# Six added split places at stage ends, no GpSimd split at mix2's entries, and a reordered first expert round

## The chip, the cores and the metric

The kernel runs on one core of a Trainium2 chip. The metric is the device time of one execution in microseconds. The kernel before takes 2223.85 us (median of 3 runs, 2223.41 to 2227.16).

## What is computed

Two blocks, one after the other, on 256 tokens of 1024 features in float32, each of depth 2.

```python
def first_block(x, mem, ...):
    for l in range(DEPTH):
        h = rms_norm(x, ffn1_norms[l, 0])
        x = x + 0.5 * rms_norm(swiglu(h, ffn1_w13[l], ffn1_w2[l]), ffn1_norms[l, 1])
        h = rms_norm(x, mix_norms[l, 0])
        y = token_mixing(h, w_in[l], ...)
        x = x + rms_norm(y, mix_norms[l, 1])
        h = rms_norm(x, cross_norms[l, 0])
        x = x + rms_norm(cross_attention(h, m, ...), cross_norms[l, 1])
        h = rms_norm(x, ffn2_norms[l, 0])
        x = x + 0.5 * rms_norm(swiglu(h, ffn2_w13[l], ffn2_w2[l]), ffn2_norms[l, 1])
def second_block(x, c, ...):
    for l in range(DEPTH):
        mod = (c_act @ w_ada[l] + b_ada[l])[:, None, :]
        shift_m, scale_m, gate_m, shift_f, scale_f, gate_f = jnp.split(mod, N_MOD, axis=-1)
        h = rms_norm_2(x, norm_mix[l]) * (1.0 + scale_m) + shift_m
        x = x + gate_m * hybrid_mixer(h, w_in[l], ...)
        h = rms_norm_2(x, norm_ffn[l]) * (1.0 + scale_f) + shift_f
        x = x + gate_f * hierarchical_moe(h, ...)   # 4 groups x 8 experts, top 2 of one group
```

## The kernel before

The tokens are two tiles of 128, t=0 and t=1. The stages follow one another: ffn1, mix, cross and ffn2 for each layer, then mix2 and the experts for each layer. A float32 product is three matmuls (`mm3`, L303 to L305): each operand is split into a high and a low half, and high x high, high x low and low x high are added up.

**Weights.** `Stream` holds a stage sequence's weights in the order of their use. `load` sends them over SP's queue, 1 MB each, into four buffers raw0 to raw3. `pump` splits them in pieces of 128x512 into places: ACT writes the high half (L288 with the norm's gain folded in, L291 without), DVE the low half (L289, L293), or GpSimd, at L293 too, where a key's third field is true and the piece's number is odd. There are eight places (SPLITS): four tiles "hl" and two tiles "pair" that hold two each. `take` hands out the next split piece after pumping as many as there are places; `release` gives a place back, and `taken` gives a raw buffer back, upon which `load` sends the next transfer. A new split needs a free place, so what may be split ahead is limited by the eight.

**The end of a stage.** `finish` calls `dense_out`, the stage's last product, and `boundary`. `dense_out` works through items of one weight piece each (six matmuls, three per tile): first the head, all but the last eight, for both tiles; then the eight tail pieces for t=0, and, handed out by `rest(n, pump)`, for t=1. In `boundary` tile 0's residual add and norm (`add_post`: L506, L508, L511) stand beside those matmuls of tile 1. Then comes `staggered`: the next stage's first product, one pass of 24 matmuls for t=0 (`run(0)`, L373 and L375), tile 1's transposes (`out_of(1)`, L446), and the same for t=1 (`run(1)`). The eight pieces for it are taken in `run(0)`; their places are released in `run(1)`. Where a gain can be folded into the weights (five ends: ffn1 to mix and cross to ffn2 in both layers, and ffn2 to ffn1 between them) x itself is transposed; else `pre_norm` makes h first (L521, L524, L529).

**mix2's entries.** `mix2_keys` marks the first two keys with True, so half of their eight low halves are written by GpSimd (eight instructions in the kernel).

**Adaptation rows.** `ada_step` sums a row of 1024 on DVE, and `close` reduces it over the partitions with two matmuls of 512 columns and adds the bias on DVE (L1342).

**Experts.** `moe` works in eight rounds q of four experts. A round gathers the tokens (L1951, evicted by ACT at L1956 and DVE at L1958), multiplies with gate and up weights (`gate_up`, L1964), weighs the result, transposes it (L2007, L2009) and multiplies with the down weights (L2021); `ymoe` (L2026) puts the rows back. Its weights come unsplit through SP's queue; transfers wait for the buffers that the gate/up and down matmuls give back (issued at L1726). The routing weights per slot come from `comb`: 16 matmuls of four columns, for all rounds, after the first round's gate/up (L1987). A float32 matmul of the expert stages leaves two records in the trace.

Of the kernel before, what the change touches and what calls it, by code (L numbers as in the profile page):

```python
# [35 lines left out]
SPLITS = 8  # L36
# [131 lines left out]
class Stream:  # L168
# [3 lines left out]
    def __init__(self, kern, keys, limit=None):  # L172
        self.kern, self.keys = kern, list(keys)
        self.raws, self.ready = [], deque()
# [4 lines left out]
        self.emitted = 0  # L179
        self.load(limit)  # L180
# [73 lines left out]
class Kernel:  # L254
# [106 lines left out]
    def staggered(self, keys, lhs):  # L361

        outs = self.mm("first")
        parts = []
        te = self.nc.tensor

        def run(t):
            for k0 in (0, 4):
                if t == 0:
                    parts.extend(self.st.take(*keys[k0 // 4]) for _ in range(4))  # L370
                for k in range(k0, k0 + 4):
                    for i in range(2):
                        te.matmul(outs[t], lhs(k, t)[0], parts[k][i], start=(k == 0 and i == 0), stop=False)  # L373
                for k in range(k0, k0 + 4):
                    te.matmul(outs[t], lhs(k, t)[1], parts[k][0], start=False, stop=(k == 7))  # L375
                    if t == 1:
                        self.st.release()
                        self.st.pump(1)

        return outs, run  # L380

    def dense_out(self, keys, lhs, tail, closing=None, mid=(), ada=None, halves=False):
# [131 lines left out]
    def pre_norm(self, x, g, sh, junk, h):  # L514
# [16 lines left out]
    def boundary(self, ys, rest, post, gp, gn, first=None, filler=None):  # L531
# [13 lines left out]
        def pre_of(t):  # L545
# [5 lines left out]
            elif gn is not None:  # L551
                self.pre_norm(self.x[t], gn[0], gn[1], *tiles[t])
# [15 lines left out]
        rest(1, 1)  # L568
        post_of(0)
        rest(1, 1)  # L570
# [6 lines left out]
        else:  # L577
            pre_of(0)
            rest(2, 2)
# [3 lines left out]
        self.st.pump(2)  # L583
# [736 lines left out]
    def ada_step(self, l, i, k, fp):  # L1320
# [4 lines left out]
        def rows():  # L1325
            bn = self.A("bn")
            for g in range(2):
                p, c0 = slice(32 * g, 32 * g + 32), g * 512
                nc.sync.dma_start(bn[p, 0, :], self.a["b_ada"][l, i * D + c0:i * D + c0 + 512].unsqueeze(0)
                                  .to_broadcast([32, 512]))  # L1330
                if gain:
                    nc.sync.dma_start(bn[p, 1, :], self.a[gain][l, c0:c0 + 512].unsqueeze(0).to_broadcast([32, 512]))
            return bn

        def close(acc, bn):

            tp = self.tp("adap")
            for g in range(2):
                nc.tensor.matmul(tp[32 * g:32 * g + 32, :], self.ones[:, 0:32], acc[:, g * 512:(g + 1) * 512],
                                 start=True, stop=True)  # L1340
            row = fp.tile([64, 512], F32, tag="row", name="row")
            nc.vector.tensor_add(row, tp[0:64, :], bn[0:64, 0, :])  # L1342
            if gain:
                nc.vector.scalar_tensor_tensor(row, row, 1.0, bn[0:64, 1, :], op0=ALU.add, op1=ALU.mult)
            for g in range(2):
                c0 = i * D + g * 512
                nc.sync.dma_start(self.mod_dram[l:l + 1, c0:c0 + 512], row[32 * g:32 * g + 1, :])
# [64 lines left out]
    def mix2_keys(self, l):  # L1412
        keys = [("win2", (l, i), True) for i in range(2)] + [("wlr", (l,), False)]
# [419 lines left out]
    def moe(self, l, hm, L, pre):  # L1833
        nc, a, tc = self.nc, self.a, self.tc
        te, ve = nc.tensor, nc.vector
        with self.moe_ctx as es:
# [78 lines left out]
            def one_round(ahead):  # L1915
# [28 lines left out]
                def gather(q, cuts=((0, 4), (4, 8)), xg=None):  # L1944
# [24 lines left out]
                with tc.manual_schedule(engines=ORDERED) if ahead else nullcontext():  # L1969
                    places(0, 4)  # L1970
                    xg = gather(0, {0: ((0, 1), (1, 2)), 1: ((2, 4),), 3: ((4, 8),)}[0])
                    for k in range(8):
# [10 lines left out]
                        if k == 7:  # L1983
                            comb_tp = self.tp("comb")
                            for i in range(8):
                                for t in range(2):
                                    te.matmul(comb_tp[:, i * 4:(i + 1) * 4], P[t][:, i * 128:(i + 1) * 128],  # L1987
                                              comb[:, t, i * 4:(i + 1) * 4], start=(t == 0), stop=(t == 1))
                            cw, cs = r2.tile([128, 8, 4], F32, name="cw"), r2.tile([128, 8], F32, name="cs")
                            ve.tensor_mul(cw, comb_tp[:, 0:32].rearrange("p (q e) -> p q e", q=8),  # L1990
                                          self.misc[:, 34:38].unsqueeze(1).to_broadcast([128, 8, 4]))
                            ve.reduce_sum(cs, cw, AX.X)
                for q in range(8):
# [10 lines left out]
                    ve.scalar_tensor_tensor(sil, sil, cs[:, q:q + 1], gu[:, 256:512], op0=ALU.mult, op1=ALU.mult)  # L2004
# [9 lines left out]
                    nc.scalar.activation(PT, tp[:, 256:512].rearrange("p (f s) -> p f s", f=2), AF.Copy)  # L2014
                    dn = self.mm("dn")
# [102 lines left out]
```

## Time and profile before

| | before |
|---|---|
| median of 3 runs | 2223.85 us |
| the profiled execution | 2221.21 us |
| its span | 2219.2 us |
| PE busy | 2108.2 us (95%) |
| DVE busy | 1350.9 us (61%) |
| ACT busy | 1157.7 us (52%) |
| GpSimd (POOL) busy | 68.4 us (3%) |
| HBM read | 549.85 MB, 248 GB/s over the span |

All durations are those of the profiled execution. Its own time is 2 us more than its span, for what lies around the span, and 2.6 us below the median. An engine's busy time counts its instructions from start to end; idle time in the timeline stands in brackets with what ended it.

### The profile page before, as it was taken

What the parts mean: (1) busy time and instruction counts of PE and PEld (TensorE: products, weight loads), DVE (VectorE), ACT (ScalarE), POOL (GpSimd) and SP (SyncE); (2) the same over time, 40 slices, a digit from 0 to 9 for tenths busy, and PEclk for the clock granted to TensorE, in tenths of its full rate; (3) what the DMA queues carried; (4) which work ended last, traced back from release to release, by engine and by line L of the source; (5) the groups of instructions that cost most, each with busy time, mean ns of one, the idle gap of its engine ahead of it and who ended that gap; (6) DMA issues with size and microseconds to landing.
All of it is one profiled execution on the core that took longest, in us unless ns stands there. A gap on an engine that the chain in (4) does not pass through costs nothing. (4 is left out here: it accounts for less than half of the span.)

```text
span 2219.2 us, 28887 instructions
## 1 busy us (share of the span) xinstructions
PE 2108.2 (95%) x10668; PEld 1561.2 (70%) x10668; DVE 1350.9 (61%) x2472; ACT 1157.7 (52%) x2196; POOL 68.4 (3%) x76
## 2 busy tenths in 40 slices
PE   8999999999999999999999999998999887998895
PEld 7887878888788788777788878876765333775341
DVE  6876767765787687676677558766562114563111
ACT  6555677565655555466766556545842112762110
POOL 0000000000000000000000000002000001100000
PEclk9999999999999999999999999999999898999998
DMA  7875534553687577744356437766489998569998
GB/s 290 315 246 203 191 117 168 192 194 128 218 286 240 201 277 260 261 169 152 133 182 225 152 126 276 261 248 242 152 315 380 418 418 331 220 240 370 418 417 338
DMA packets 94551, 552.96 MB, mean 249 GB/s; under 512 B 11223, under 2 KB 12954, under 8 KB 41398
## 3 DMA queue, kind: packets, MB, share of 16 engines
q1 hardware_dynamic: 94398, 550.99, 67.0%
q8 instruction: 88, 1.44, 0.3%
q14 instruction: 65, 0.53, 0.1%
HBM read 549.85 MB, written 1.10 MB: 248 GB/s over the span
## 5 line engine op out<-in xcount | busy, mean ns | idle before, releaser
L289 DVE SCALAR_TENSOR_TENSOR hl<-raw,g_pre,hl 128x512 fp32r<-128x512 f32 (+1 forms) x296 | 214.2, 744 | 46.1 <-ACT hl L288 45.6
L288 ACT ACTIVATE hl<-raw,g_pre 128x512 fp32r<-128x512 f32 (+1 forms) x296 | 204.5, 719 | 62.4 <-PE gu L305 24.9
L289 DVE SCALAR_TENSOR_TENSOR pair<-raw,g_pre,pair 128x512 fp32r<-128x512 f32 (+1 forms) x296 | 207.6, 744 | 46.1 <-ACT pair L288 43.5
L293 DVE TENSOR_TENSOR hl<-raw,hl 128x512 fp32r<-128x512 f32 (+1 forms) x286 | 192.7, 688 | 68.8 <-ACT hl L291 65.5
L288 ACT ACTIVATE pair<-raw,g_pre 128x512 fp32r<-128x512 f32 (+1 forms) x296 | 196.6, 715 | 71.8 <-PE gu L305 52.0
L291 ACT ACTIVATE hl<-raw 128x512 fp32r<-128x512 f32 (+1 forms) x290 | 176.9, 626 | 94.3 <-PE y L305 41.1
L1964 PE MATMUL gu<-raw,xg 128*32 128x512 f32 x1024 | 144.0, 633 | 25.2 <-DMA raw<-w_gu 23.0
L293 DVE TENSOR_TENSOR pair<-raw,pair 128x512 fp32r<-128x512 f32 (+1 forms) x184 | 119.8, 692 | 69.7 <-ACT pair L291 69.3
L291 ACT ACTIVATE pair<-raw 128x512 fp32r<-128x512 f32 (+1 forms) x188 | 107.4, 621 | 91.6 <-PE y L305 64.3
L303 PE MATMUL gu<-pair,hh 128*128 128x512 f32 x320 | 127.3, 398 | 0.0
L303 PE MATMUL gu<-hl,hh 128*128 128x512 f32 x320 | 126.3, 395 | 0.0
L305 PE MATMUL gu<-pair,hl 128*128 128x512 f32 x320 | 125.1, 391 | 0.0
L305 PE MATMUL gu<-hl 128*128 128x512 f32 x320 | 125.0, 391 | 0.0
L304 PE MATMUL gu<-pair,hh 128*128 128x512 f32 x320 | 124.8, 390 | 0.0
L304 PE MATMUL gu<-hl,hh 128*128 128x512 f32 x320 | 124.8, 390 | 0.0
L1359 DVE SCALAR_TENSOR_TENSOR ada<-raw,cact,ada 128x512 f32<-128x512 f32 x168 | 122.0, 745 | 0.0
L1964 PEld LDWEIGHTS gu<-raw,xg 128*32 128x32 f32 x1024 | 29.8, 112 | 107.2 <-DMA raw<-w_gu 52.9
L1951 PEld LDWEIGHTS gather<-P,u 128*128 128x128 f32 x512 | 69.0, 214 | 30.3 <-issue 21.3
L2021 PE MATMUL dn<-raw,aT 128*32 128x512 f32 x512 | 79.2, 623 | 10.2 <-DMA raw<-w_dn 3.0
L2004 DVE SCALAR_TENSOR_TENSOR sil<-sil,cs,gu 128x256 f32<-128x256 f32 x16 | 7.7, 481 | 124.0 <-ACT sil L2003 123.7
L298 DVE TENSOR_TENSOR y<-dn,y 128x512 fp32r<-128x512 f32 x32 | 22.1, 692 | 98.5 <-ACT y L297 98.4
L1956 ACT ACTIVATE xg<-gather,fm 128x128 f32<-128x128 f32 x64 | 29.2, 457 | 95.4 <-PE gather L1951 80.6
(672 smaller groups left out, 4879.3 us busy)
## 6 DMA issues: line engine op xcount, KB each, us to landing
raw<-w SPq DMA_DIRECT2D x131, 1024.0 KB
raw<-w_gu SPq DMA_DIRECT2D x98, 1024.0 KB
raw<-win SPq DMA_DIRECT2D x71, 1024.0 KB
raw<-w_dn SPq DMA_DIRECT2D x54, 1024.0 KB
raw<-w_ada SPq DMA_DIRECT2D x48, 1024.0 KB
raw<-w_gu SPq DMA_DIRECT2D x60, 512.0 KB
raw<-w_out SPq DMA_DIRECT2D x16, 1024.0 KB
raw<-cross_wkv SPq DMA_DIRECT2D x16, 1024.0 KB
```

Of the source, the lines that this page charges most:

```text
L288: nc.scalar.activation(hi, raw[:, c0:c0 + n], AF.Copy, scale=gain)
L289: nc.vector.scalar_tensor_tensor(lo, raw[:, c0:c0 + n], gain, hi.bitcast(F32), op0=ALU.mult, op1=ALU.subtract)
L291: nc.scalar.activation(hi, raw[:, c0:c0 + n], AF.Copy)
L293: eng.tensor_tensor(out=lo, in0=raw[:, c0:c0 + n], in1=hi.bitcast(F32), op=ALU.subtract)
L303: te.matmul(out, xh, wh, start=start, stop=False)
L304: te.matmul(out, xh, wl, start=False, stop=False)
L305: te.matmul(out, xl, wh, start=False, stop=stop)
L1359: nc.vector.scalar_tensor_tensor(self.ada[:, c], w, act, self.ada[:, c], op0=ALU.mult, op1=ALU.add)
L1951: te.matmul(ps[:, (k - k0) * 128:(k - k0 + 1) * 128], hm[t][:, k * 128:(k + 1) * 128], P[t][:, q * 128:(q + 1) * 128], start=(t == 0), sto ...
L1956: nc.scalar.activation(xg[:, k, :], v, AF.Identity, bias=sh, scale=g)
L1964: te.matmul(gu[32 * e:32 * e + 32, :], xg[:, k, 32 * e:32 * e + 32], w(e), start=(k == 0), stop=(k == 7))
L2021: te.matmul(dn[half][32 * e:32 * e + 32, :], aT[:, f, 32 * e:32 * e + 32], w(e), start=(f == 0), stop=(f == 1))
```

## The change

It consists of five parts.

1. In the last six head items of a stage that has a next stage's first product (`AHEAD`), each item allows one extra split place, a tile "ahead" from the pool "ap". It serves the five folded ends and the entry of mix2 in layer 0. During the pass for t=0 (`held`) `take` pumps no more than it needs.
2. In `boundary` the numbers handed to `pump` move: fewer pieces between the residual instructions, one piece ahead of h's scaling, and all that is missing of eight ahead of x[1]'s last add where nothing is folded.
3. The first two keys of mix2 are no longer marked for GpSimd.
4. `ada_step` closes a row in four groups of 256 columns on 128 partitions instead of two of 512 on 64.
5. In `moe` the comb matmuls are made round by round (two each), the next round's gather is emitted after the transposes are evicted instead of before them, and one eviction of the first gather goes to ACT.

```diff
-SPLITS = 8
+SPLITS, AHEAD = 8, 6
...
     def slot(self, i):
...
+        if self.extra:
+            self.extra -= 1
+            self.used.append(None)
+            return self.kern.ap.tile([128, 2, 512], F32R, tag="A", name="ahead").rearrange("p a b -> p (a b)")
...
     def take(self, name, index):
-        self.pump()
+        self.pump(SPLITS if not self.held else 0 if self.ready else 1)
...
         def run(t):
+            self.st.held = t == 0
...
-        for k, c in items[:head]:
+        for i, (k, c) in enumerate(items[:head]):
+            if i >= head - ahead:
+                self.st.extra += 1
...
     def pre_norm(self, x, g, sh, junk, h, between=None):
...
+        if between:
+            between()
         for c in HALF:
...
         post_of(0)
-        rest(1, 1)
+        rest(1, int(fold))
         post_of(0)
-        rest(1, 1)
+        rest(1, int(fold))
...
         else:
-            pre_of(0)
-            rest(2, 2)
+            pre_of(0, lambda: self.st.pump(1))
+            rest(2)
             rest(4)
             post_of(1)
             out_of(0)
-        self.st.pump(2)
+        if fold or ys is None:
+            self.st.pump(2)
+        else:
+            self.st.pump(8 - len(self.st.ready))
         post_of(1)
...
-        ys, rest = self.dense_out(keys, lhs, tail, closing, mid, ada, experts)
+        ys, rest = self.dense_out(keys, lhs, tail, closing, mid, ada, experts, 0 if kw.get("first") is None else AHEAD)
...
-            for g in range(2):
-                nc.tensor.matmul(tp[32 * g:32 * g + 32, :], self.ones[:, 0:32], acc[:, g * 512:(g + 1) * 512],
+            for g in range(4):
+                nc.tensor.matmul(tp[32 * g:32 * g + 32, 0:256], self.ones[:, 0:32], acc[:, g * 256:(g + 1) * 256],
                                  start=True, stop=True)
-            row = fp.tile([64, 512], F32, tag="row", name="row")
-            nc.vector.tensor_add(row, tp[0:64, :], bn[0:64, 0, :])
+            row = fp.tile([128, 256], F32, tag="row", name="row")
+            nc.vector.tensor_add(row, tp[:, 0:256], bn[:, 0, 0:256])
...
-        keys = [("win2", (l, i), True) for i in range(2)] + [("wlr", (l,), False)]
+        keys = [("win2", (l, i), False) for i in range(2)] + [("wlr", (l,), False)]
...
-                            if k % 2 == 0:
+                            if k % 2 == 0 or (first and k == 1):
...
-                        if k == 7:
-                            comb_tp = self.tp("comb")
-                            for i in range(8):
-                                for t in range(2):
-                                    te.matmul(comb_tp[:, i * 4:(i + 1) * 4], P[t][:, i * 128:(i + 1) * 128],
-                                              comb[:, t, i * 4:(i + 1) * 4], start=(t == 0), stop=(t == 1))
...
-                    if q < 7:
-                        xg = gather(q + 1)
+                    ctp, cw, cs = self.tp("comb"), r2.tile([128, 4], F32, name="cw"), r2.tile([128, 1], F32, name="cs")
+                    for t in range(2):
+                        te.matmul(ctp[:, 0:4], P[t][:, q * 128:(q + 1) * 128], comb[:, t, q * 4:(q + 1) * 4],
+                                  start=(t == 0), stop=(t == 1))
+                    ve.tensor_mul(cw, ctp[:, 0:4], self.misc[:, 34:38])
+                    ve.reduce_sum(cs, cw, AX.X)
...
                     nc.scalar.activation(PT, tp[:, 256:512].rearrange("p (f s) -> p f s", f=2), AF.Copy)
+                    if q < 7:
+                        xg = gather(q + 1)
                     dn = self.mm("dn")
```

**How the rows move.** The first place is DVE at the end of ffn1 in layer 0, before the change (x_85 and x_86 are x for t=0 and t=1; g_pre marks the next stage's weights; y is the last product).

```order
L293 TENSOR_TENSOR hl<-raw,hl 128x512 x3
L506 TENSOR_TENSOR u<-y_1287,gain 128x512
L464 TENSOR_SCALAR rs_tmp<-ms 128x1
L508 TENSOR_TENSOR u<-y_1288,gain 128x512
L511 SCALAR_TENSOR_TENSOR x_85<-u,rs,x_85 128x512 x2
L289 SCALAR_TENSOR_TENSOR pair<-raw,g_pre,pair 128x512 x3
L298 TENSOR_TENSOR hl<-tp,hh 128x512 x2
L506 TENSOR_TENSOR u<-y_1289,gain 128x512
L464 TENSOR_SCALAR rs_tmp<-ms 128x1
L508 TENSOR_TENSOR u<-y_1290,gain 128x512
L289 SCALAR_TENSOR_TENSOR pair<-raw,g_pre,pair 128x512
L289 SCALAR_TENSOR_TENSOR hl<-raw,g_pre,hl 128x512
```

The same place in the changed kernel, from one extra place on to the first pair of x_86:

```order
L298 TENSOR_TENSOR ahead<-raw,ahead 128x512
L294 SCALAR_TENSOR_TENSOR hl<-raw,g_pre,hl 128x512
L1356 TENSOR_TENSOR row<-adap,bn 128x256
L294 SCALAR_TENSOR_TENSOR ahead<-raw,g_pre,ahead 128x512
L294 SCALAR_TENSOR_TENSOR hl<-raw,g_pre,hl 128x512
L294 SCALAR_TENSOR_TENSOR ahead<-raw,g_pre,ahead 128x512
L294 SCALAR_TENSOR_TENSOR hl<-raw,g_pre,hl 128x512 x2
L515 TENSOR_TENSOR u<-y_1301,gain 128x512
L473 TENSOR_SCALAR rs_tmp<-ms 128x1
L517 TENSOR_TENSOR u<-y_1302,gain 128x512
L520 SCALAR_TENSOR_TENSOR x_85<-u,rs,x_85 128x512 x2
L294 SCALAR_TENSOR_TENSOR pair<-raw,g_pre,pair 128x512 x2
```

Before, the eight splits of the next stage (g_pre) all stand behind x_85's add, the last three behind x_86's. Now six of them stand ahead of the first `u`, and two behind x_85's add.

The second place is PE in the first round of the experts. Before, 16 comb rows and 14 gather rows stand ahead of these:

```order
L1951 MATMUL gather<-P_14179,u 128x128
L1951 MATMUL gather<-P_14180,u 128x128
L2007 MATMUL actT<-ident,sil 128x128 x2
L2009 MATMUL actT<-ident,P_14179 128x128
L2009 MATMUL actT<-ident,P_14180 128x128
L1964 MATMUL gu<-raw,xg 32x512 x5
L2021 MATMUL dn_14341<-raw,aT 32x512 x8
L1964 MATMUL gu<-raw,xg 32x512 x4
L2026 MATMUL ymoe_14181<-y,PT 128x512
```

In the changed kernel two comb rows and nine gather rows stand ahead of these:

```order
L1965 MATMUL gather<-P_14268,u 128x128
L1965 MATMUL gather<-P_14267,u 128x128
L2015 MATMUL actT<-ident,sil 128x128 x2
L2017 MATMUL actT<-ident,P_14267 128x128
L2017 MATMUL actT<-ident,P_14268 128x128
L1965 MATMUL gather<-P_14268,u 128x128
L1965 MATMUL gather<-P_14267,u 128x128
L1965 MATMUL gather<-P_14268,u 128x128
L1965 MATMUL gather<-P_14267,u 128x128
L1965 MATMUL gather<-P_14268,u 128x128
L2031 MATMUL dn_14415<-raw,aT 32x512 x8
L1978 MATMUL gu<-raw,xg 32x512
```

The four transposes now come in the middle of the gather, and the first down matmuls (dn) stand directly behind it; the gate/up matmuls that stood around them come later.

The third place is DVE at the entry of mix2 in layer 0, before the change (hl and pair from raw are the splits; h is what PE transposes).

```order
L511 SCALAR_TENSOR_TENSOR x_85<-u,rs,x_85 128x512 x2
L293 TENSOR_TENSOR pair<-raw,pair 128x512
L521 TENSOR_TENSOR h<-x_85,gain 128x512
L464 TENSOR_SCALAR rs_tmp<-ms 128x1
L524 TENSOR_TENSOR h<-x_85,gain 128x512
L529 SCALAR_TENSOR_TENSOR h<-h,rs,gain 128x512 x2
L293 TENSOR_TENSOR pair<-raw,pair 128x512
L506 TENSOR_TENSOR u<-y_12476,gain 128x512
L464 TENSOR_SCALAR rs_tmp<-ms 128x1
L508 TENSOR_TENSOR u<-y_12477,gain 128x512
L298 TENSOR_TENSOR hl<-tp,hh 128x512 x2
L293 TENSOR_TENSOR hl<-raw,hl 128x512
```

In the changed kernel:

```order
L298 TENSOR_TENSOR ahead<-raw,ahead 128x512
L298 TENSOR_TENSOR pair<-raw,pair 128x512 x2
L515 TENSOR_TENSOR u<-y_12558,gain 128x512
L473 TENSOR_SCALAR rs_tmp<-ms 128x1
L517 TENSOR_TENSOR u<-y_12559,gain 128x512
L520 SCALAR_TENSOR_TENSOR x_85<-u,rs,x_85 128x512 x2
L530 TENSOR_TENSOR h<-x_85,gain 128x512
L473 TENSOR_SCALAR rs_tmp<-ms 128x1
L533 TENSOR_TENSOR h<-x_85,gain 128x512
L540 SCALAR_TENSOR_TENSOR h<-h,rs,gain 128x512 x2
L515 TENSOR_TENSOR u<-y_12560,gain 128x512
L473 TENSOR_SCALAR rs_tmp<-ms 128x1
```

The three splits ahead of `u` take the place of those between the instructions that make h, and the four low halves that GpSimd wrote stand on DVE.

## Rows read from the trace of the kernel before

**Rows 1.** The page's first section: engine, busy us, share of the span, instructions.

```profile
PE 2108.2 (95%) x10668; PEld 1561.2 (70%) x10668; DVE 1350.9 (61%) x2472; ACT 1157.7 (52%) x2196; POOL 68.4 (3%) x76
```

**Rows 2.** Timeline, PE, 758 to 775: start us, us, instruction, count, [idle before <-releaser].

```profile
758.56 1.09 PE L373 MATMUL first<-pair,hh 128*128 128x512 f32 x4
...
766.83 1.03 PE L446 MATMUL tp<-ident,x 128*128 128x128 f32 x8
768.12 1.21 PE L373 MATMUL first<-pair,hh 128*128 128x512 f32 x4 [0.25 <-ACT hh L297]
...
773.73 0.39 PE L303 MATMUL gu<-pair,hh 128*128 128x512 f32 x1
```

**Rows 3.** Timeline, PE, the end of layer 0's cross stage.

```profile
564.16 1.07 PE L373 MATMUL first<-hl,hh 128*128 128x512 f32 x4
...
569.83 1.16 PE L373 MATMUL first<-hl,hh 128*128 128x512 f32 x3 [1.26 <-DVE hl L289]
...
571.75 1.04 PE L446 MATMUL tp<-ident,x 128*128 128x128 f32 x8
```

**Rows 4.** Timeline, DVE, the same end: the adds that make x[1].

```profile
567.70 1.41 DVE L511 SCALAR_TENSOR_TENSOR x<-u,rs,x 128x512 f32<-128x512 f32 x2
```

**Rows 5.** Windows: stretch, us, busy time of PE, PEld, DVE, ACT, POOL, clock, DMA share, GB/s.

```profile
531.00:552.00 21.00, 20.31 (x100) 16.91 (x98) 10.74 (x24) 10.07 (x23) 0.00 (x0) 1.00 0.30 101
```

**Rows 6.** The page's groups: busy us, mean ns | idle before, releaser.

```profile
L289 DVE SCALAR_TENSOR_TENSOR hl<-raw,g_pre,hl 128x512 fp32r<-128x512 f32 (+1 forms) x296 | 214.2, 744 | 46.1 <-ACT hl L288 45.6
L288 ACT ACTIVATE hl<-raw,g_pre 128x512 fp32r<-128x512 f32 (+1 forms) x296 | 204.5, 719 | 62.4 <-PE gu L305 24.9
...
L293 DVE TENSOR_TENSOR hl<-raw,hl 128x512 fp32r<-128x512 f32 (+1 forms) x286 | 192.7, 688 | 68.8 <-ACT hl L291 65.5
```

**Rows 7.** Timeline, PE, entry of mix2 in layer 0.

```profile
1509.91 1.29 PE L446 MATMUL tp<-ident,h 128*128 128x128 f32 x8 [1.77 <-DVE h L529]
...
1513.78 0.51 PE L373 MATMUL first<-pair,hh 128*128 128x512 f32 x1 [0.65 <-POOL pair L293]
...
1518.31 0.96 PE L373 MATMUL first<-hl,hh 128*128 128x512 f32 x3 [1.96 <-DVE hl L293]
...
1520.93 1.29 PE L446 MATMUL tp<-ident,h 128*128 128x128 f32 x8 [0.74 <-DVE h L529]
```

**Rows 8.** Timeline, DVE, the same entry: the two scalings of h (t=0, t=1).

```profile
1508.03 2.41 DVE L529 SCALAR_TENSOR_TENSOR h<-h,rs,gain 128x512 f32<-128x512 f32 x2 [0.44 <-POOL rs L465]
...
1520.03 1.41 DVE L529 SCALAR_TENSOR_TENSOR h<-h,rs,gain 128x512 f32<-128x512 f32 x2 [0.45 <-POOL rs L465]
```

**Rows 9.** Timeline, DVE, entry of mix2 in layer 1.

```profile
1866.30 2.36 DVE L293 TENSOR_TENSOR hl<-raw,hl 128x512 fp32r<-128x512 f32 x2
...
1869.78 3.10 DVE L293 TENSOR_TENSOR pair<-raw,pair 128x512 fp32r<-128x512 f32 x2
```

**Rows 10.** Timeline, PE, first round of the second expert stage.

```profile
2019.95 3.73 PE L1987 MATMUL comb<-comb,P 128*128 128x4 f32 x32
2023.54 3.82 PE L1951 MATMUL gather<-P,u 128*128 128x128 f32 x32
2027.20 0.38 PE L2007 MATMUL actT<-ident,sil 128*128 128x128 f32 x2
...
2028.70 0.63 PE L2021 MATMUL dn<-raw,aT 128*32 128x512 f32 x3
```

**Rows 11.** Windows of the expert stages, columns as in rows 5.

```profile
1640.00:1680.00 40.00, 34.96 (x261) 24.53 (x259) 18.17 (x68) 13.89 (x30) 1.11 (x2) 0.87 0.86 340
2000.00:2035.00 35.00, 29.17 (x224) 17.33 (x226) 14.24 (x59) 9.18 (x18) 0.56 (x1) 0.90 0.90 343
2035.00:2080.00 45.00, 43.77 (x315) 20.38 (x308) 9.09 (x19) 8.96 (x19) 0.00 (x0) 1.00 1.01 417
```

**Rows 12.** SP's waits, 2000 to 2035: us in total, times, longest us.

```profile
SPq L1726 <- PE dn L2021: 10.0, 2, 9.6
```

**Rows 13.** The chain that ended last, in order of time: start us, us, what.

```profile
2195.75 12.57 DMA raw<-w_dn
```

More of the change, by code (lines that the diff above doesn't have):

```diff
@@ L173, in __init__ @@
         self.kern, self.keys = kern, list(keys)
-        self.raws, self.ready = [], deque()
+        self.raws, self.ready, self.held = [], deque(), False
         self.free, self.tags = deque(RAWS), []
@@ L178, in __init__ @@
                       for s, (c0, n) in enumerate(SEGMENTS.get(key[0], [(j * 512, 512) for j in range(4)]))]
-        self.emitted = 0
+        self.emitted = self.extra = 0
         self.load(limit)
@@ L378, in run, with dense_out @@
                         self.st.pump(1)
+            self.st.held = False
         return outs, run
-    def dense_out(self, keys, lhs, tail, closing=None, mid=(), ada=None, halves=False):
+    def dense_out(self, keys, lhs, tail, closing=None, mid=(), ada=None, halves=False, ahead=0):
         ys = [self.mm("y%d" % t) for t in range(2)]
@@ L512, in add_post, with pre_norm @@
         yield
-    def pre_norm(self, x, g, sh, junk, h):
+    def pre_norm(self, x, g, sh, junk, h, between=None):
         nc = self.nc
@@ L543, in boundary, with pre_of @@
             self.pre = self.small.tile([128, 2], F32, tag="pre", name="pre", bufs=2)
-        def pre_of(t):
+        def pre_of(t, between=None):
             if fold:
@@ L551, in pre_of @@
             elif gn is not None:
-                self.pre_norm(self.x[t], gn[0], gn[1], *tiles[t])
+                self.pre_norm(self.x[t], gn[0], gn[1], *tiles[t], between)
         def out_of(t):
@@ L1326, in rows @@
             bn = self.A("bn")
-            for g in range(2):
-                p, c0 = slice(32 * g, 32 * g + 32), g * 512
-                nc.sync.dma_start(bn[p, 0, :], self.a["b_ada"][l, i * D + c0:i * D + c0 + 512].unsqueeze(0)
-                                  .to_broadcast([32, 512]))
+            for g in range(4):
+                p, c0 = slice(32 * g, 32 * g + 32), g * 256
+                nc.sync.dma_start(bn[p, 0, 0:256], self.a["b_ada"][l, i * D + c0:i * D + c0 + 256].unsqueeze(0)
+                                  .to_broadcast([32, 256]))
                 if gain:
-                    nc.sync.dma_start(bn[p, 1, :], self.a[gain][l, c0:c0 + 512].unsqueeze(0).to_broadcast([32, 512]))
+                    nc.sync.dma_start(bn[p, 1, 0:256], self.a[gain][l, c0:c0 + 256].unsqueeze(0).to_broadcast([32, 256]))
             return bn
@@ L1337, in close @@
             tp = self.tp("adap")
-            for g in range(2):
-                nc.tensor.matmul(tp[32 * g:32 * g + 32, :], self.ones[:, 0:32], acc[:, g * 512:(g + 1) * 512],
+            for g in range(4):
+                nc.tensor.matmul(tp[32 * g:32 * g + 32, 0:256], self.ones[:, 0:32], acc[:, g * 256:(g + 1) * 256],
                                  start=True, stop=True)
-            row = fp.tile([64, 512], F32, tag="row", name="row")
-            nc.vector.tensor_add(row, tp[0:64, :], bn[0:64, 0, :])
+            row = fp.tile([128, 256], F32, tag="row", name="row")
+            nc.vector.tensor_add(row, tp[:, 0:256], bn[:, 0, 0:256])
             if gain:
[L1344 to L1347, printed above, removed]
+                nc.vector.scalar_tensor_tensor(row, row, 1.0, bn[:, 1, 0:256], op0=ALU.add, op1=ALU.mult)
+            for g in range(4):
+                c0 = i * D + g * 256
+                nc.sync.dma_start(self.mod_dram[l:l + 1, c0:c0 + 256], row[32 * g:32 * g + 1, :])
             yield 0
@@ L1942, in places, with gather @@
                                          op=ALU.is_equal)
-                def gather(q, cuts=((0, 4), (4, 8)), xg=None):
+                def gather(q, cuts=((0, 4), (4, 8)), xg=None, first=False):
                     if xg is None:
@@ L1970, in one_round @@
                     places(0, 4)
-                    xg = gather(0, {0: ((0, 1), (1, 2)), 1: ((2, 4),), 3: ((4, 8),)}[0])
+                    xg = gather(0, {0: ((0, 1), (1, 2)), 1: ((2, 4),), 3: ((4, 8),)}[0], first=True)
                     for k in range(8):
@@ L1982, in one_round @@
                                 ve.tensor_copy(cint, cmax)
-                        if k == 7:
-                            comb_tp = self.tp("comb")
-                            for i in range(8):
-                                for t in range(2):
-                                    te.matmul(comb_tp[:, i * 4:(i + 1) * 4], P[t][:, i * 128:(i + 1) * 128],
-                                              comb[:, t, i * 4:(i + 1) * 4], start=(t == 0), stop=(t == 1))
[L1989 to L1992, printed above, removed]
                 for q in range(8):
@@ L1999, in one_round @@
                         self.spread(l, pre)
[L2000 to L2001 removed]
+                    ctp, cw, cs = self.tp("comb"), r2.tile([128, 4], F32, name="cw"), r2.tile([128, 1], F32, name="cs")
[4 more added lines that the diff above has]
+                    ve.reduce_sum(cs, cw, AX.X)
                     sil = r2.tile([128, 256], F32, tag="sil", name="sil", bufs=1)
                     nc.scalar.activation(sil, gu[:, 0:256], AF.Silu)
[L2004 removed]
+                    ve.scalar_tensor_tensor(sil, sil, cs, gu[:, 256:512], op0=ALU.mult, op1=ALU.mult)
                     tp = self.tp("actT")
```

## Prediction

> **What bounds the kernel now.** I read the page's first section, then the stretches between two stages (timelines of PE and DVE), then the two expert stages (windows, SP's waits, chain). PE is busy for 2108.2 of the 2219.2 us [rows 1], so only time in which PE sits still, or in which it is not what limits, can be won. Two kinds of such time show up.
>
> The first is the end of a stage. The last tile's matmuls run, and the next stage's `first` matmuls start before their weights are split. At one end the first pass (24 matmuls, t=0) runs from 758.56 to 766.83, which is 8.27 us; the second pass, the same 24 matmuls with the weights lying ready, runs from 768.12 to 773.73, which is 5.61 us [rows 2]. The difference, 2.66 us, is waiting for splits, as the end in rows 3 shows: its first pass takes from 564.16 to 571.75, 7.59 us, so 1.98 us more than with ready weights, and 1.26 us of that is one wait for a low half that DVE writes at L289 [rows 3]. There are five such ends whose gain is folded in the weights: two of 8.27 us and three of 7.6 us by the same view.
>
> The second kind is the first round of each expert stage. DMA moves 340 and 343 GB/s in the stretches 1640 to 1680 and 2000 to 2035, and 417 GB/s from 2035 on [rows 11]. From there to the end the experts' weights set the pace: the chain of waits ends in the w_dn transfer that lands 12.57 us after 2195.75 [rows 13], with some 10 us of work behind it. A byte not moved in the first round is paid for at the end.
>
> **Folded ends (AHEAD).** Six more places let six more of the next stage's weights be split during the last head items, before the tail fills ACT and DVE. With all weights ready the five first passes last 5.61 us each: 2 x 8.27 + 3 x 7.60 - 5 x 5.61 = 11.3 us to win. What is late next is x[1], whose transpose follows the pass. At the end of rows 3 its two L511 adds start at 567.70 and last 1.41 us [rows 4], so x[1] is there at 569.1, against a pass that would end at 564.16 + 5.61 = 569.8: 0.7 us to spare, and more where fewer splits stand ahead of it on DVE.
>
> The splits are not new, they are moved ahead: one costs ACT 0.719 us and DVE 0.744 us [rows 6]. Six of them are 4.3 us and 4.5 us in a head that leaves DVE 21 - 10.74 = 10.3 us and ACT 10.9 us free over 21 us [rows 5], so on the average they fit. Packed into six items they nearly saturate both engines: an item is six matmuls, about 1.4 us of PE (24 matmuls take 5.61 us), and holds one own and one extra split, 2 x 0.744 = 1.49 us of DVE. In the two cross heads softmax uses both as well. I take 0.4 us of lateness at each of these two, 0.8 us together; the bounds are 0 and, where all of the extra DVE time lands there, 4.5 us each. Term: -10.5 us.
>
> **mix2 entry of layer 0.** It gets the extra places and loses the GpSimd halves. PE waits 1.77 us for h, 0.65 us for a GpSimd half, 1.96 us for a DVE half, and 0.74 us more ahead of the second transpose, 5.1 us in all [rows 7]. Of the 1.77 us, 1.00 us is a stretched instruction: the two L529 scalings took 2.41 us while a GpSimd split ran, 1.41 us at 1520.03 without one [rows 8]. The splits' waits go if the weights are split early: 1.00 + 0.65 + 1.96 = 3.6 us; of the 0.74 us I take half. Term: -4.0 us, bounds -5.1 and -2.0 (only the later split's wait).
>
> **mix2 entry of layer 1.** No extra places here, since the expert stage precedes it; only the four GpSimd halves become DVE's. That adds 4 x 0.688 = 2.75 us on DVE [rows 6]. Against it, DVE pairs were stretched while GpSimd worked: two pairs of L293 took 2.36 and 3.10 us [rows 9] where twice the mean of 0.688 is 1.38, so 2.7 us, and with 1.00 us for the L529 pair as in rows 8 it is 3.7 us. Term: -1.0 us, bounds -3.7 and +2.75.
>
> Here a rule of the Trainium skill speaks against the change. Perfetto Trace Analysis, section Optimizing Scalar/DVE Operations, says that where DVE is saturated, handing some work to Scalar or even to GpSimd may make sense (it adds that the two share a read port, so that it might not help). By the first half of this, the term would be +2.75 us at each entry; by the rows, the stretching costs more than the halves do, and the measurement is what I go by.
>
> **Expert stages.** In the second, PE runs the 16 small comb matmuls (two records each) from 2019.95, gathers from 2023.54 for 3.82 us, then the transposes and some gate/up matmuls, and reaches the first down matmul at 2028.70 [rows 10], 8.75 us after comb's start. SP, which must reuse the buffers that the down matmuls free, waits 9.6 us for L2021 at a time [rows 12], and this is the stretch in which DMA falls short. After the change two comb matmuls (2/16 of 3.6, 0.45 us), the gathers (3.82), four transposes (0.5 us; the first two take 0.38 us) and no gate/up stand before it: 4.8 us, 4.0 us earlier. The first stage has the same pattern. The k=1 eviction on ACT may let the first gate/up start a little sooner; I count it in the bounds alone, as it lies ahead of SP's wait.
>
> What DMA can give back is bounded by the shortfall: 40 x (1 - 340/417) = 7.4 us and 35 x (1 - 343/417) = 6.2 us. I take 4.0 us of each stage, since a transfer that starts 4.0 us earlier ends as much earlier if the queue is full from there on, as it is [rows 11]. Bounds: 0 and 13.6 us for both. The comb matmuls of the later rounds fall where PE waits for DMA anyway. Term: -8.0 us.
>
> **The rest.** The adaptation rows are added as 128x256 instead of 64x512 (0.68 us, twelve times, nobody waits for more than a row long due), with two more small matmuls and a few more small DMAs on SP each. The cover is the head's matmuls, 1.4 us per item; if it is gone, 12 x 0.5 us. Term 0.
>
> **Sum.** -10.5 - 4.0 - 1.0 - 8.0 = -23.5 us against the profiled execution's 2221.2 us gives 2197.7 us. The median of the runs shown is 2.6 us above that execution, so on its scale **2200 us**. A change of 0.2%, 4.4 us, is about what a measurement of this kernel can tell from none.
>
> **Rivals.**
> 1. DMA gives nothing back (chance 0.16). The w_gu waits of SP, not those for L2021, would then set the pace, or the late gathers push the next round's gate/up back by as much. For it: SP waits for gate/up matmuls too in this stretch. Against: the longest single wait is L2021's [rows 12]. 2200.3 + 8.0 = 2208 us.
> 2. Both cross heads choke (0.08): the extra splits there delay the head by their DVE time, 2 x 6 x 0.744 = 8.9 us in place of 0.8, and the 4.0 us won at these two ends are lost: 2200.3 + 4.0 + 8.1 = 2212 us. For it: two splits an item saturate DVE; against: half of DVE is free in this stretch [rows 5].
> 3. All of it comes back (0.10): the DMA's 13.6 us and both entries' upper bounds, 5.1 and 3.7 us: 2200.3 - 5.6 - 1.1 - 2.7 = 2191 us.
> 4. GpSimd's halves were a help (0.03). DVE writes what PE waits for at both entries, so every added half ends up in front of PE: 2 x 2.75 us in place of -5.0: 2200.3 + 10.5 = 2211 us. Against: rows 8 and 9. This is what the rule quoted above would do here.
> 5. Slower (0.03): in the last six items each extra split makes the head's own next split late, since ACT's half and DVE's half follow each other, 0.719 + 0.744 = 1.46 us, and PE has nothing else to run. At six ends that is 36 splits. It decides from (23.5 + 4.4) / 36 = 0.78 us of PE time per split on; at 1.1 us, between one half and both, it is 2200.3 + 39.6 = 2240 us. For it: the engines are full for six items. Against: eight places lie ahead of PE when the extra ones begin, a reserve of several items.
> 6. Cases 1, 2 and 4 together (0.03): 2200.3 + 8.0 + 12.1 = 2220 us, no change that can be told.
>
> **How the numbers follow.** The forecast, with its terms some 3 us off either way in sum, has 0.57, the rivals the rest. The range runs from 2191 us (case 3) to 2212 us (cases 1, 2, 4), which leaves out 5 and 6, half of case 3 and a part of case 2: 0.15. Faster by over 0.2%: all but cases 5 and 6, 0.94; within 0.2%: case 6, 0.03; slower: case 5, 0.03.
>
> **What would show it.** Right: first passes of 5.6 to 6.0 us at the five ends, and hardly any idle time of `first` until L294 halves; no GpSimd split at the mix2 entries, L540 pairs of 1.4 us; the first down matmul some 4.8 us after the first comb matmul, SP's longest wait for down matmuls near 5.6 us, and over 370 GB/s in the first rounds. Wrong: PE gaps before y matmuls in the last six head items (rivals 2, 5), waits of the tp transposes for x[1], first rounds that end earlier with the last w_dn landing no earlier relative to them (rival 1), or DVE pushing h back at layer 1's entry (rival 4).

## The result and the profile after

The changed kernel takes 2192.99 us (median of 4 runs, 2189.84 to 2193.95) against 2224.26 us: ratio 0.9853, 95% interval 0.9837 to 0.9868. That is 31 us less, inside the range of the forecast and 7 us below its 2200 us. The profiled execution took 2189.84 us, its span is 31.2 us shorter than before.

The page's first section of the changed kernel, span and engines:

```profile
span 2188.0 us, 29032 instructions
...
PE 2090.5 (96%) x10716; PEld 1555.2 (71%) x10716; DVE 1346.8 (62%) x2506; ACT 1158.7 (53%) x2198; POOL 54.6 (2%) x68
```

PE is busy 17.7 us less [rows 1], and POOL, without its eight splits, 54.6 us instead of 68.4 us. Where the time came from is read off the timelines of PE, by the start of the same instruction in both kernels:

| start of | before | after | gained so far |
|---|---|---|---|
| first pass, ffn1 to mix, layer 0 | 204.41 | 202.43 | 1.98 |
| first pass, cross to ffn2, layer 0 | 564.16 | 560.04 | 4.12 |
| first pass, ffn2 to ffn1 | 758.56 | 751.06 | 7.50 |
| first pass, ffn1 to mix, layer 1 | 953.66 | 942.07 | 11.59 |
| first pass, cross to ffn2, layer 1 | 1314.44 | 1300.39 | 14.05 |
| first pass, mix2, layer 0 | 1511.23 | 1492.48 | 18.75 |
| mix2's last product, layer 0 | 1618.70 | 1596.71 | 21.99 |
| last `ymoe`, layer 0 | 1858.39 | 1832.80 | 25.59 |
| first pass, mix2, layer 1 | 1867.28 | 1841.13 | 26.15 |
| mix2's last product, layer 1 | 1972.03 | 1944.35 | 27.68 |
| end of the span | 2219.2 | 2188.0 | 31.2 |

The first 20 us hold 0.7 us of the first row. They are not the change's: among runs whose code is the same there, this stretch varies by up to 1.9 us.

**The folded ends.** Timeline of PE in the changed kernel, the end of layer 0's cross stage (columns as in rows 2):

```profile
560.04 0.62 PE L379 MATMUL first<-hl,hh 128*128 128x512 f32 x2
...
565.51 1.04 PE L455 MATMUL tp<-ident,x 128*128 128x128 f32 x8
```

The first pass lasts 565.51 - 560.04 = 5.47 us where it lasted 7.59 us [rows 3]. By the same view all five last 5.46 or 5.47 us, 27.3 us together against 39.4 us.

**mix2's entries.** Timeline of PE in the changed kernel, layer 0 (beside rows 7):

```profile
1491.17 1.29 PE L455 MATMUL tp<-ident,h 128*128 128x128 f32 x8 [0.45 <-DVE h L540]
...
1499.67 1.29 PE L455 MATMUL tp<-ident,h 128*128 128x128 f32 x8 [1.46 <-DVE h L540]
```

The two waits for splits are gone. The first wait for h fell from 1.77 to 0.45 us; the second grew from 0.74 to 1.46 us. Timeline of DVE in the changed kernel, layer 0 and then layer 1:

```profile
1490.27 1.41 DVE L540 SCALAR_TENSOR_TENSOR h<-h,rs,gain 128x512 f32<-128x512 f32 x2 [0.44 <-POOL rs L474]
...
1498.77 1.42 DVE L540 SCALAR_TENSOR_TENSOR h<-h,rs,gain 128x512 f32<-128x512 f32 x2 [0.44 <-POOL rs L474]
```

```profile
1839.73 1.89 DVE L298 TENSOR_TENSOR hl<-raw,hl 128x512 fp32r<-128x512 f32 x3
...
1843.34 1.88 DVE L298 TENSOR_TENSOR pair<-raw,pair 128x512 fp32r<-128x512 f32 x3
```

The L540 pair for t=0 takes 1.41 us where it took 2.41 us [rows 8], and three splits in layer 1 take 1.89 and 1.88 us where two took 2.36 and 3.10 us [rows 9].

**The first expert round.** Timeline of PE in the changed kernel, second expert stage, then the windows of both first rounds (columns as in rows 5) and SP's waits from 1975 to 2010 (columns as in rows 12):

```profile
1991.22 0.61 PE L2006 MATMUL comb<-comb,P 128*128 128x4 f32 x4
...
1995.87 1.92 PE L2031 MATMUL dn<-raw,aT 128*32 128x512 f32 x16
```

```profile
1616.00:1656.00 40.00, 35.70 (x255) 21.80 (x254) 20.63 (x72) 15.84 (x32) 1.11 (x2) 0.91 0.91 362
1972.00:2007.00 35.00, 30.70 (x220) 15.67 (x223) 14.68 (x61) 10.66 (x20) 0.56 (x1) 0.90 0.97 388
```

```profile
SPq L1740 <- PE dn L2031: 10.0, 4, 5.3
```

From the first comb matmul to the first down matmul it is 4.65 us, 8.75 us before [rows 10]; SP's longest wait for a down matmul is 5.3 us instead of 9.6 us [rows 12], and DMA moves 362 and 388 GB/s instead of 340 and 343 [rows 11]. The window of 362 GB/s begins 2 us earlier in its stage than that of rows 11; from 1618 to 1658, the same place in the stage, it is 379 GB/s.

**What the forecast had at nothing.** The PE group of the adaptation rows, before and then after (columns as in rows 6):

```profile
L1339 PE MATMUL adap<-ada,ones 128*32 128x512 f32 x48 | 12.6, 605 | 0.0
```

```profile
L1353 PE MATMUL adap<-ada,ones 128*32 128x256 f32 x96 | 7.7, 391 | 0.0
```

4.9 us less for the same columns. Aligned instruction by instruction, the two timelines of PE draw apart by 0.41 us at each of the twelve closings.

### The profile page after: what moved, and what is told of

Its sections match the earlier page's. It is cut to its first block, busy times and chain, and to the rows that moved or that the text cites. A ratio compares the mean times of both kernels' runs of the same rounds, so it can differ in the third digit from the quotient of the medians.

```text
span 2188.0 us, 29032 instructions
## 1 busy us (share of the span) xinstructions
PE 2090.5 (96%) x10716; PEld 1555.2 (71%) x10716; DVE 1346.8 (62%) x2506; ACT 1158.7 (53%) x2198; POOL 54.6 (2%) x68
## 5 line engine op out<-in xcount | busy, mean ns | idle before, releaser
L294 DVE SCALAR_TENSOR_TENSOR pair<-raw,g_pre,pair 128x512 fp32r<-128x512 f32 (+1 forms) x290 | 203.6, 744 | 56.5 <-ACT pair L293 54.9
L293 ACT ACTIVATE hl<-raw,g_pre 128x512 fp32r<-128x512 f32 (+1 forms) x292 | 203.1, 718 | 64.0 <-PE gu L310 24.9
L298 DVE TENSOR_TENSOR hl<-raw,hl 128x512 fp32r<-128x512 f32 (+2 forms) x274 | 183.4, 683 | 64.5 <-ACT hl L296 61.8
L296 ACT ACTIVATE hl<-raw 128x512 fp32r<-128x512 f32 (+2 forms) x274 | 167.2, 625 | 79.9 <-PE y L310 30.8
L298 DVE TENSOR_TENSOR pair<-raw,pair 128x512 fp32r<-128x512 f32 (+1 forms) x178 | 114.3, 684 | 60.6 <-ACT pair L296 60.3
L296 ACT ACTIVATE pair<-raw 128x512 fp32r<-128x512 f32 (+1 forms) x178 | 102.0, 622 | 84.5 <-PE y L310 55.8
L2011 ACT ACTIVATE sil<-gu 128x256 f32<-128x256 f32 x16 | 6.1, 383 | 137.4 <-PE gu L1978 137.4
L1965 PE MATMUL gather<-P,u 128*128 128x128 f32 x512 | 71.6, 290 | 5.2 <-DVE xg L1972 3.7
```

The source lines that it names most:

```text
L293: nc.scalar.activation(hi, raw[:, c0:c0 + n], AF.Copy, scale=gain)
L294: nc.vector.scalar_tensor_tensor(lo, raw[:, c0:c0 + n], gain, hi.bitcast(F32), op0=ALU.mult, op1=ALU.subtract)
L296: nc.scalar.activation(hi, raw[:, c0:c0 + n], AF.Copy)
L298: eng.tensor_tensor(out=lo, in0=raw[:, c0:c0 + n], in1=hi.bitcast(F32), op=ALU.subtract)
L1965: te.matmul(ps[:, (k - k0) * 128:(k - k0 + 1) * 128], hm[t][:, k * 128:(k + 1) * 128], P[t][:, q * 128:(q + 1) * 128], start=(t == 0), sto ...
```

## The experiments

Each was made from the changed kernel unless it says otherwise. Ratios are to the kernel before, each interval about 0.0017 to either side except where given; 0.001 is 2.2 us. A distance between two medians is good to about 2 us, since the kernel before, measured beside each, took 2224.3 to 2226.3 us. Two kernels whose intervals overlap are told apart by their timelines of PE, which from one stage to the next agree within a few tenths of a us where the code and the granted clock are the same (the first 20 us of the kernel vary by up to 1.9 us, the expert stages by 1.8 us).

**e1, closings as before.** The lines of `ada_step` are those of the kernel before, among them:

```diff
-            for g in range(4):
-                nc.tensor.matmul(tp[32 * g:32 * g + 32, 0:256], self.ones[:, 0:32], acc[:, g * 256:(g + 1) * 256],
+            for g in range(2):
+                nc.tensor.matmul(tp[32 * g:32 * g + 32, :], self.ones[:, 0:32], acc[:, g * 512:(g + 1) * 512],
```

> The changed kernel with the adaptation rows closed as before (two groups of 512 columns on 64 partitions). Theory (the four 32-column groups run side by side on PE, so each of the 12 closings is 0.41 us shorter for the matmuls behind it): 12 x 0.41 = 4.9 us above the changed kernel, about 2198 us, adap records back at 1.05 us per closing. Rival (the prediction's own price, the closings are hidden and the 0.41 us steps come from something else in the stage): within 1 us of the changed kernel, about 2193 us.

Measured: ratio 0.9882, 2199.55 us. The timeline loses 0.41 us or a little more at each closing, 5.2 us in all. The profiled spans lie 9.6 us apart; the rest is 1.6 us by a lower clock in one pass (last section), 2.2 us in the expert stages, within the spread given at e3, and 0.7 us in the first 20 us. The theory holds.

**e6, four matmuls into two groups.**

```diff
-            for g in range(4):
-                nc.tensor.matmul(tp[32 * g:32 * g + 32, 0:256], self.ones[:, 0:32], acc[:, g * 256:(g + 1) * 256],
+            for b in range(2):
+                for g in range(2):
+                    c0 = g * 512 + b * 256
+                    nc.tensor.matmul(tp[32 * g:32 * g + 32, b * 256:b * 256 + 256], self.ones[:, 0:32],
+                                     acc[:, c0:c0 + 256], start=True, stop=True)
```

> The changed kernel with each adaptation row closed by four matmuls of 256 columns, as in the change, but written to two groups of 32 partitions instead of four. Theory (matmuls into different groups of 32 partitions overlap on PE): a closing takes about 1.0 us of PE again, 12 x 0.42 = 5.0 us above the changed kernel, the steps of 0.42 us standing at the twelve closings. Rival (shorter matmuls are what helps): 0.64 us per closing and no step.

Measured: ratio 0.9877 (0.9856 to 0.9899), 2196.94 us. The group of e6:

```profile
L1355 PE MATMUL adap<-ada,ones 128*32 128x256 f32 x96 | 12.7, 385 | 0.0
```

The matmuls are as many and as long as in the change, and busy time is back at 12.7 us; a closing takes 1.06 us. So it is the four groups of 32 partitions, not the shorter matmuls. The Trainium skill, TensorE: Matmul & The Clock Gate, Part 3 (Packing small matmuls), says that the array can be addressed in tiles of 32 by 32 and can run several small matmuls at once, and that a column tile's output is a group of 32 partitions. These rows agree, 12.7 to 7.7 us from two groups to four.

**e2, no extra places.**

```diff
-SPLITS, AHEAD = 8, 6
+SPLITS, AHEAD = 8, 0
```

> The changed kernel with no extra split places, the moved pump numbers kept. Theory (the places are what makes the first passes short): the five folded first passes are back at 7.6 to 8.3 us, 11.3 us lost, 0.9 us of lateness in one cross head won back, some 1 to 2 us lost at mix2's entry in layer 0: 10 to 13 us above the changed kernel, 2203 to 2206 us. Rival (the moved pump numbers and the held pass do the work, eight places are enough): less than 4 us above, under 2197 us.

Measured: ratio 0.9924, 2209.11 us. Timeline of PE, the same end:

```profile
563.45 1.07 PE L379 MATMUL first<-hl,hh 128*128 128x512 f32 x4
...
569.12 1.16 PE L379 MATMUL first<-hl,hh 128*128 128x512 f32 x3 [1.25 <-DVE hl L294]
...
571.04 1.03 PE L455 MATMUL tp<-ident,x 128*128 128x128 f32 x8
```

7.59 us again, with the wait for the DVE half back; all five as before, 39.3 us. That is 16.1 us above the change, more than the 10 to 13 us expected. Aligned with the change, 11.8 us lie in the first block, 3.1 us at mix2's entry and 1.3 us in a pass at a lower clock (last section). The moved pump numbers alone give the folded ends nothing; whether the places need them was not tried.

**e12 and e13, two and three places** (e13 with 3 in the same line).

```diff
-SPLITS, AHEAD = 8, 6
+SPLITS, AHEAD = 8, 2
```

> The changed kernel with two extra places instead of six at all six stage ends. Theory (each missing place leaves one more split to stand beside the pass, and half of them can be hidden behind it, as three places hid all at the cross ends): the five folded first passes, 5.5 us with six places and 7.6 to 8.3 us with none, come out between 5.5 and 6.8 us; 1 to 6 us above the changed kernel. Rival (all six are needed): first passes near 7.4 us, 8 us or more above.

> The changed kernel with three extra places instead of six at all six stage ends. Theory: first passes of 5.5 us at all five folded ends, as at the two cross ends with three, mix2's entry in layer 0 within 1 us: within 1.5 us of the changed kernel. Rival (the ends of ffn1 and ffn2, whose first passes waited longest, need all six): 0.7 us or more lost at each of those three ends, 2 us or more above.

Measured: 0.9881 and 0.9872 (0.9855 to 0.9888), 2199.87 and 2196.95 us. With two places the first passes last 6.94, 5.46, 5.46, 6.94 and 5.46 us; with three, all last 5.46 us. So the folded ends need three, and there the rival falls. The 6.94 us and the 6.9 us above the change are a little more than expected of two places. At mix2's entry three are short: waits of 0.5 us for a split and 2.46 instead of 1.46 us for the second h, 1.9 us in the timeline, more than the 1 us expected. e13 lies 4.0 us above the change, not within 1.5 us; besides the entry its profile has 1.6 us by a lower clock in one pass (last section).

**e11, three places in the cross stages alone.**

```diff
-0 if kw.get("first") is None else AHEAD)
+0 if kw.get("first") is None else 3 if keys[0][0] == "cross_wo" else AHEAD)
```

> The changed kernel with three extra places instead of six in the two cross stages. Theory (the six splits lie in front of ACT's softmax there): PE's wait for pt at L1271 in layer 0 falls from 1.55 to at most 1.1 us, and with three places fewer some 0 to 2 us of the first pass's waits come back at each of the two ends: between 1 us below and 3 us above the changed kernel. Rival (the wait at L1271 is not the splits'): it stays at 1.55 us, and only the first passes change.

Measured: 0.9863 (0.9846 to 0.9879), 2194.07 us, the first passes still 5.46 us. PE's wait ahead of co in layer 0, six places and then three:

```profile
546.20 1.99 PE L1294 MATMUL co<-pt,V 128*128 128x256 f32 x8 [1.55 <-ACT pt L1271]
```

```profile
546.08 1.99 PE L1294 MATMUL co<-pt,V 128*128 128x256 f32 x8 [1.23 <-ACT pt L1271]
```

The same wait in the timelines of all these runs, in us:

| extra places in the cross stages | layer 0 | layer 1 |
|---|---|---|
| none (kernel before, e2) | 0.69 | 0.69 |
| two (e12) | 0.69 | 0.69 |
| three (e11) | 1.23 | 1.57 |
| three (e13) | 1.75 | 1.23 |
| six (the change) | 1.55 | 0.95 |

So three or six places delay the softmax and two do not, but the delay does not follow their number: in e11 the wait fell in layer 0, by less than expected, and grew in layer 1. The rival falls, and the theory's relief is not shown; which order of splits makes the delay stays open. The kernel's time is not told apart from the change's.

**e3, expert stages as before.** Its edit is those of e7, e8 and e9 below together.

> The changed kernel with the expert stages as before (all comb matmuls ahead, the gather ahead of the transposes, k=1 evicted on DVE). Theory (the first round's down matmuls come 4 us late and DMA never makes that up): 4.1 + 3.5 = 7.7 us above the changed kernel, about 2201 us, SP's longest wait for the down matmuls back near 10 us. Rival (the weights' transfers set the pace either way, and the gain at the end came from the earlier start of the stage): less than 3 us above, under 2196 us.

Measured: 0.9886, 2200.69 us, so 7.7 us above the change; SP's longest wait for a down matmul in the second stage is 11.5 us, the down matmuls come 24.93 us after the first gather instead of 18.1 us, and the stages, first gather to last `ymoe`, last 206.8 and 208.5 us instead of 202.7 and 202.3 us (206.3 and 205.8 us in the kernel before). The runs whose expert code is that of the change spread from 202.2 to 204.0 us.

**e7, e8, e9, its three parts undone one by one**, in this order:

```diff
                         self.spread(l, pre)
+                    if q < 7:
+                        xg = gather(q + 1)
...
-                    if q < 7:
-                        xg = gather(q + 1)
                     dn = self.mm("dn")
```

```diff
+                        if k == 7:
+                            comb_tp = self.tp("comb")
+                            for i in range(8):
...
-                    ctp, cw, cs = self.tp("comb"), r2.tile([128, 4], F32, name="cw"), r2.tile([128, 1], F32, name="cs")
...
```

```diff
-                            if k % 2 == 0 or (first and k == 1):
+                            if k % 2 == 0:
```

> The changed kernel with the next round's gather emitted ahead of the silu and the transposes, as before; comb stays round by round. Theory (the long comb was what held the first down matmuls back): first comb or gather to first down matmul within 0.5 us of the changed kernel's 4.65 us, total within 1.5 us of it. Rival (the place of the gather carries it): 3 us later in each stage, 6 to 8 us above the changed kernel.

> The changed kernel with all 16 comb matmuls ahead of the first round's gather, as before; the gather's later place stays. Theory: the first down matmuls come 14/16 x 3.6 = 3.1 us later in each stage and the transfers behind them too, 6 us above the changed kernel. Rival (the gather's place carries it): under 1.5 us above.

> The changed kernel with the first gather's k=1 eviction on DVE, as before. Theory: PE's wait ahead of the third gate/up group is back at 0.7 us in the first and 1.5 us in the second stage, the down matmuls come as much later, and DMA never makes it up: 1 to 2.3 us above the changed kernel. Rival: the wait is back but lies ahead of what DMA waits for, 0 us.

| | ratio (interval) | first gather to first down | stages |
|---|---|---|---|
| change | 0.9853 (0.9837 to 0.9868) | 18.04, 18.16 us | 202.7, 202.3 us |
| e7, gather early | 0.9853 (0.9832 to 0.9874) | 19.98, 20.11 us | 202.9, 203.1 us |
| e8, comb ahead | 0.9879 (0.9857 to 0.9902) | 21.99, 21.95 us | 206.7, 204.6 us |
| e9, k=1 on DVE | 0.9866 (0.9845 to 0.9888) | 19.21, 19.21 us | 203.6, 202.8 us |

The comb matmuls carry most of the gain: e8 lies 5.1 us above the change, its stages are 4.0 and 2.3 us longer (2.7 and 0.6 us above the spread). The gather's place delays the down matmuls by 1.9 us, more than the 0.5 us expected, and costs nothing that can be told. The eviction delays them by 1.1 us (they come after 18.0 to 18.8 us in the runs with the change's expert code), and its stages lie within the spread, so that neither its theory nor its rival is decided. Why 1.9 us are free and 3.9 us are not stays open; SP's longest wait is 6.4 us in e7 and 8.5 us in e8.

**e4, GpSimd's halves back.**

```diff
-        keys = [("win2", (l, i), False) for i in range(2)] + [("wlr", (l,), False)]
+        keys = [("win2", (l, i), True) for i in range(2)] + [("wlr", (l,), False)]
```

> The changed kernel with half of the low halves at mix2's entries on GpSimd again. Theory (a GpSimd split stretches the DVE instructions beside it): 1.5 us lost at layer 1's entry, 1 to 3 us at layer 0's, where the splits now lie earlier: 2.5 to 4.5 us above the changed kernel, 2195.5 to 2197.5 us, and DVE pairs of 2 us and more beside GpSimd's splits. Rival (the rule that a busy DVE is helped by handing work to GpSimd): 2 us or more below the changed kernel, under 2191 us.

Measured: 0.9859 (0.9843 to 0.9876), 2194.44 us, not told apart from the change. Timeline of DVE, then of GpSimd, at layer 1's entry:

```profile
1841.39 3.44 DVE L540 SCALAR_TENSOR_TENSOR h<-h,rs,vector 128x512 f32<-128x512 f32 x2
```

```profile
1841.25 3.03 POOL L298 TENSOR_TENSOR hl<-raw,hl 128x512 fp32r<-128x512 f32 x2
```

The pair that makes h takes 3.44 us instead of 1.41 us while GpSimd splits; PE's wait for h grows from 5.87 to 7.08 us there, and by 0.42 us for the second h in layer 0, where one GpSimd split runs beside x[1]'s adds. From layer 0's last `ymoe` to the first matmul behind the two passes of layer 1's entry (`lrt`) it is 23.95 us instead of 21.98 us; the kernel before has 24.05 us. The sign is as expected, the size smaller: the extra places already cover most of layer 0's entry.

**e10, the kernel before without GpSimd's halves, nothing else** (the diff of e4 the other way round, on the kernel before).

> The kernel before with one edit, mix2's first two keys no longer marked for GpSimd. Theory (a GpSimd split stretches the DVE instructions beside it, and without the extra places this stands in PE's way): 1.5 to 3.5 us off layer 0's entry and 1 to 1.5 us off layer 1's, 3 to 5 us below the kernel before. Rival (a busy DVE is helped by GpSimd): up to 5.5 us above it.

Measured: 0.9983 (0.9973 to 0.9993; 10 runs), 2221.12 us, 3.8 us below the kernel before. Timeline of DVE at layer 0's entry, the pair that makes x[1] in the kernel before, then both pairs in e10:

```profile
1514.20 3.46 DVE L511 SCALAR_TENSOR_TENSOR x<-u,rs,x 128x512 f32<-128x512 f32 x2
```

```profile
1507.50 1.42 DVE L529 SCALAR_TENSOR_TENSOR h<-h,rs,gain 128x512 f32<-128x512 f32 x2 [0.44 <-POOL rs L465]
...
1513.75 1.41 DVE L511 SCALAR_TENSOR_TENSOR x<-u,rs,x 128x512 f32<-128x512 f32 x2
```

Both pairs take 1.4 us, where they took 2.41 us [rows 8] and 3.46 us. Aligned with the kernel before, 1.5 us are gained at layer 0's entry, and layer 1's, measured as in e4, takes 22.47 us instead of 24.05 us. So handing halves to GpSimd was a cost here, and the rival falls. The Trainium skill, SBUF — State Buffer, section Who interferes with whom, says that a DVE instruction with two SBUF inputs contends with a GpSimd instruction that reads SBUF; the stretched pairs agree.

No run beat the change by more than its interval.

## Why the prediction was right, and where it was short

The signs and places of the four terms were right, and a fifth term was missing. Between the profiled executions the forecast, -23.5 us, is 7.7 us short of 31.2 us: the closings give 4.9 us of that, the folded ends 1.3, mix2's two entries 0.6 and 1.1, the first 20 us 0.7 us, which is spread, and the expert stages take 0.9 us back.

- Folded ends, -10.5: the passes gave 12.0 us, 0.7 us more than ready weights were thought to give, since the first passes last 5.46 us and not the 5.61 us of the second pass that was taken for them. The softmax was late by 0.86 and 0.26 us at the two cross ends, 1.1 us where 0.8 us were forecast; all in all the term came to 11.8 us. x[1] was never waited for.
- mix2's entry of layer 0, -4.0: 4.6 us (21.99 less the 17.4 us gained up to its last y). The sum came out better than its parts: the first wait for h fell by 1.32 us, not 1.00, and of the 0.74 us nothing was won, that wait grew. The pair of x[1], stretched to 3.46 us (e10), was not in the forecast. Either cause alone carries a part: 1.5 us without GpSimd (e10), 3.1 us lost without the places (e2), 0.4 us with GpSimd back (e4).
- Layer 1, -1.0: 2.1 us (27.68 less 25.59). With GpSimd back 2.0 us of it are lost (e4), and without GpSimd alone 1.6 us are gained (e10), so rival 4 falls. A part comes by way of the clock, which the forecast did not count: the granted clock was 0.50 in the first 4.0 us of the first pass before (1867.28 to 1871.30), and 0.76 in its first 2.5 us after (1841.10 to 1843.60). In both PE had waited about 6 us for h; before, it waited another 0.59 us in the middle of the transposes.
- Expert stages, -8.0: 3.6 and 3.5 us. The signs named for it came: 4.65 us to the first down matmul, 5.3 us for SP's longest wait, 379 and 388 GB/s. Rival 1 falls with e3. That the term came out near its size is in part luck. It let each us by which the down matmuls come earlier shorten the stage by one; counted from the first gather they came 6.9 and 5.1 us earlier, and the gather's place, credited with a share, gave nothing that e7 shows. The comb matmuls gave most of it.
- "The rest. Term 0" is the step that failed. It priced DVE's addition and took the head's matmuls for its cover; the closing's own matmuls it did not price. They run on PE, and there nothing covers them: aligned, the timelines draw apart at each of the twelve closings. Two matmuls of 512 columns a closing cost 12.6 us in all, and the four groups made 4.9 us of it free. This term is most of the 7 us between forecast and result.
- Rival 2 had a mechanism that exists, but its price was 1.1 us, not 8.9 us (table at e11). Of rival 5 the timelines show nothing: at the ends of ffn1 and ffn2 nothing is lost between the stage's last closing and the first pass behind it. Rival 3's time nearly came out (2191 us forecast), but not by its way: the first rounds still fall short of 417 GB/s.

## What to carry to other kernels

Where one engine is busy for 95% of the span, price each instruction on it at its full time, unless it falls where that engine waits. Here small matmuls on it paid when their outputs were spread over four groups of 32 partitions (4.9 us), and when they were put off to later rounds (about 5 us). Count how many pieces ahead a stage end really needs (three at the folded ends here, more at mix2's entry) before giving it places, and look at what a DVE instruction costs beside a GpSimd one before handing over work.

## What was not expected of the hardware

The second pass at mix2's entry in layer 0 is the same code in the change and in e1. The windows of it, the change and then e1 (columns as in rows 5):

```profile
1501.00:1506.50 5.50, 5.50 (x24) 4.51 (x25) 3.42 (x6) 3.44 (x7) 0.00 (x0) 1.00 0.98 373
```

```profile
1506.87:1513.80 6.93, 6.93 (x23) 5.60 (x24) 3.42 (x6) 3.44 (x7) 0.00 (x0) 0.75 0.78 306
```

The granted clock was 1.00 in the one and 0.75 in the other, a part of the pass at 1.2 instead of 2.4 GHz, and the 24 matmuls took 1.4 us longer. In both, PE had just waited for h. e2, e4, e8, e12 and e13 show the same slow stretch, the kernel before (1.00) does not, nor do the other runs. So a single profile of this kernel can be some us better or worse than another at such a place, and the median of the changed kernel lies 3 us above its profiled execution.
